# A fourth chunk with seven products in the first pairs of the late stages, and the token-side forms of these stages on GpSimd

## The chip, the core and the metric

The kernel runs on one core of a Trainium2 chip. The core has TensorE (matmuls, PE in the profile, its weight loads PEld), VectorE (DVE), ScalarE (ACT), GpSimd (POOL) and SyncE (SP), which issues most of the DMAs. The metric is the device time of one execution in microseconds; the time before is the median of three runs.

## The reference

A pre-norm encoder layer on x of 256 tokens by 2048, all in float32, batch 1, one layer:

```
h    = rms_norm(x, norm_g)
proj = h @ w_in                    # cut into q, k, v, o, za, gates, xb, zb, ga, gb
ya   = mlstm(q, k, v, gates, both directions) * head_g * sigmoid(o) * silu(za)
yb   = rglru(conv(xb), both directions) * silu(zb)
merged = sigmoid(ga) * (ya @ w_branch_a) + sigmoid(gb) * (yb @ w_branch_b)
out  = rms_norm(x + merged @ w_out, final_g)
```

w_branch_a, w_branch_b, w_out and the blocks of w_in for ga and gb are all 2048 by 2048. What is changed concerns the four products with w_branch_b, gb, ga and w_branch_a, in this order: the late stages, called WB, GB, GA and WA here.

## The kernel before

**A product in three matmuls.** Each float32 value is split into a high part (a cast to the matmul type) and a low part (the value less the high one). A product of activations a (hi) and b (lo) with weights wh and wl is three matmuls: a·wh (L174), a·wl (L176), b·wh (L177). The activations are prepared once; the weights come from memory in chunks of 128 partitions by 1024 columns (two k tiles of a block of 512 output columns) and are split on the way: a DMA into a raw buffer (L133, SyncE), a cast on ScalarE (L140), a subtraction on VectorE (L141).

**Pairs.** `pair` computes two blocks of 512 columns together, over eight chunks of k (kq 0 to 7), placed at eight places in the order of the work. Each late stage has 2048 columns, so two pairs; they are called first and second pair. A chunk is done in one of two ways:
- plain (`plain`): for each of the two blocks a load, a cast, a subtraction, and 12 matmuls (two k tiles, two halves of the tokens, three matmuls): 24 matmuls a place.
- products (`products`): the 2x2 scheme with seven products in place of eight: 7x3 = 21 matmuls. It takes two loads (L190, L191), four sums of weights on VectorE (L199, L200, L203, L204, 512 columns each, into the buffers t), casts on ScalarE of b (512 columns) and of three chunks of 1024 columns (the two sums and the second block itself, all L180), and their low parts on VectorE (L181). On the token side it needs a form.

The tuples S_… give the chunks of a stage's first and second pair that use products, and L_… the places at which these chunks are put; the other chunks fill the other places in order.

**The end of a pair.** Four of the seven products go to auxiliary banks of PSUM (aux), the rest to the banks of the pair (acc). Behind the last product place the four are folded into the outputs by a copy on ScalarE (L252) and four additions on VectorE (L253 to L256). Places up to the last product place are done for both blocks together; the places behind it are done for one block first and then for the other. At the end of each block its bank is added (L262) and the stage's epilogue runs.

**Forms.** `make_form` (L271 to L285) builds what the products need of a chunk's activations: the sum of high and low part where the full value is no longer there (L277, 512 columns, for h and ya), four sums of 128 columns (L280 to L283) in a temporary tile xp, of which there is one, then a cast on ScalarE (L284) and the low part (L285, 512 columns). All of it but the cast is on VectorE. There are seven such forms for the late stages: three of yb (b forms, from sg, while sg is at hand), one of h (the other two that GB and GA use, of chunks 4 and 0, were made for earlier stages and stay in the slots F4 and F0), three of ya. They lie in four slots of the tile PT.

**Buffers.** Weight chunks go through six raw buffers, four high and four low ones, used in turn; b goes through two, and each t through one. A load into a raw buffer waits until the subtraction that read the buffer six loads before is done.

**What sets the order.** The program is written in the order of the work, but a list scheduler orders the instructions of each engine. Loads, casts, subtractions and sums of weights stand in `urgent()` blocks, which raise their priority, earlier written ones first. Each engine then runs its instructions in that order, and waits at the first one whose operands or buffer aren't ready.

Of the kernel before, what the change touches and what calls it, by code (L numbers as in the profile page):

```python
# [10 lines left out]
F32R = mybir.dt.float32r  # L11
AF = mybir.ActivationFunctionType
ALU = mybir.AluOpType
# [6 lines left out]
NB = 512  # L20
# [3 lines left out]
EPS = 1e-6  # L24
NEG = -1e30

S_WB, S_GB, S_GA, S_WA = [((0, 2, 4), (0, 2, 4))] * 4
S_OZ = (((4, 0), (2, 4)), ((4,), (1,)), ((4, 0), (2, 5)), ((4, 0), (0, 2)))
S_V = (((4,), (4,)), ((4,), (4,)))
S_WO = (0, 1, 2, 4)  # L30
L_WB, L_GB, L_GA, L_WA = ((0, 2, 4), (0, 2, 4)), ((0, 2, 4), (0, 2, 4)), ((0, 2, 4), (0, 2, 4)), ((0, 2, 4), (1, 3, 5))
L_WO = (0, 2, 4, 6)
H_FORMS = (4, 0)
PLAN = (dict(Y=('c0', '', '', 'c1',),
# [12 lines left out]
def f(ap):  # L47
    return ap.bitcast(F32)
# [3 lines left out]
def hybrid_encoder(ctx: ExitStack, tc: tile.TileContext, x, xt, pk, bif, fg, wg, wi, wr, wa, wb, wo, out):  # L52
    nc = tc.nc
    pe, act, dve, pool, sp = nc.tensor, nc.scalar, nc.vector, nc.gpsimd, nc.sync
# [10 lines left out]
    def name(n):  # L65
        uid[0] += 1
        return f"{n}_{uid[0]}"
# [4 lines left out]
    def sl(tag, dt=F32, cols=4096):  # L72
        return slot.tile([P, cols], dt, tag=tag, name=name("s" + tag))
# [41 lines left out]
    def drain():  # L115
        while queue or any(lanes):
            tick()
        lanes.clear()
# [149 lines left out]
    def halves(t, i):  # L268
        return t[:, i * 1024:i * 1024 + NB], t[:, i * 1024 + NB:(i + 1) * 1024]

    def make_form(fm, full=None, parts=None, temp=None):  # L271
        u = xp.rearrange("p a b -> p (a b)") if temp is None else temp
        if full is None:
            full = u[:, NB:2 * NB]
            hi, lo = parts
            v = full if len(hi.shape) == 2 else full.rearrange("p (k s) -> p k s", s=S)
            dve.tensor_add(v, f(hi), f(lo))  # L277
        a11, a21, a12, a22 = [full[:, i * P:(i + 1) * P] for i in range(4)]
        s1, s2, s3, s4 = [u[:, i * P:(i + 1) * P] for i in range(4)]
        dve.tensor_add(s1, a21, a22)  # L280
        dve.tensor_sub(s2, s1, a11)
        dve.tensor_sub(s3, a11, a21)
        dve.tensor_sub(s4, a12, s2)  # L283
        act.copy(fm[0], u[:, :NB])  # L284
        dve.tensor_sub(fm[1], u[:, :NB], f(fm[0]))  # L285

    def block_first(src, xhi, xlo, pre=()):
        ps, _ = acc_pair()
# [17 lines left out]
    def half_tr(src, half, after=None, turn=False):  # L306
        ps, both = acc_pair()
        for kq in range(4):
            tick()
            hi, lo = load_chunk(src[half * 4 + kq])  # L310
            tiles = [(kq * 4 + kk, m, kk * S + m * P) for kk in range(4) for m in range(2)]
            for high in (False, True) if turn and kq % 2 else (True, False):
                for k, m, o in tiles:
                    if high:
                        pe.matmul(ps[m], hi[:, o:o + P], hl_t[:, 2 * k * S:2 * (k + 1) * S],  # L315
                                  start=(k == 0), stop=(turn and k == KT - 1), skip_group_check=True)
                    else:
                        pe.matmul(ps[m][:, :S], lo[:, o:o + P], hhi(k * S, (k + 1) * S),  # L318
                                  start=False, stop=(not turn and k == KT - 1), skip_group_check=True)
            if after:  # L320
                after(kq)
        return both.rearrange("p (m q s) -> p m q s", m=2, q=2)
# [467 lines left out]
    def h_parts(kq):  # L790
        h4 = hl_t[:, kq * 4 * S:(kq + 1) * 4 * S].rearrange("p (k q s) -> p k q s", q=2, s=S)
        return [h4[:, :, q, :] for q in range(2)]

    def forms_h(kq):
        make_form(hf[kq], parts=h_parts(kq), temp=rg["hs"][:, 3072:])
# [94 lines left out]
    yah, yal = Cols([yas["h"]], 4096), Cols([yas["l"]], 4096)  # L890
    ybh, ybl = [], []
    fslot = {}
    fm_t = []

    def form(x, kq, i, **kw):
        fslot[x, kq] = halves(fm_t[0], i)
        make_form(fslot[x, kq], **kw)

    def h_form(kq, i):
        form("h", kq, i, parts=h_parts(kq))  # L900

    def ya_form(kq, i):
        form("a", kq, i, parts=[t(kq * NB, (kq + 1) * NB) for t in (yah, yal)])

    def forms(x):
        return {kq: v for (n, kq), v in fslot.items() if n == x}
# [3 lines left out]

    k_yb, k_h, k_ya = (sorted(set(sum(v, ()))) for v in (S_WB, S_GB + S_GA, S_WA))
    k_h = [kq for kq in k_h if kq not in hf]
    early = [lambda kq=kq, i=i: h_form(kq, i) for kq, i in zip(k_h, (3, 0, 1))]
    early += [lambda kq=kq, i=i: ya_form(kq, i) for kq, i in zip(k_ya[:1], (3, 0, 1)[len(early):])]

    for j in range(4):
        for i in range(2):
            both = half_tr(wi[BLK_ZB + j], i)
            if i == 0:
                zt = hp.tile([P, 2 * NB], F32, tag="zz" if j else "vhi", name=name("zt"))  # L920
                sg = hp.tile([P, 2 * NB], F32, tag="to" if j else "vlo", name=name("sg"))
            fold(zt[:, i * NB:(i + 1) * NB], both)
        act.activation(sg, zt, AF.Silu)
        dve.tensor_mul(sg, sg, hs[:, j * 1024:(j + 1) * 1024])
        ybh.append(sl(f"C{j}", F32R, 1024))
        ybl.append(sl(f"D{j}", F32R, 1024))
        act.copy(ybh[j], sg)
        dve.tensor_sub(ybl[j], sg, f(ybh[j]))
        if j == 0:
            fm_t.append(sl("PT", F32R))  # L930
        if j == 0:
            drain()
        for kq in (2 * j, 2 * j + 1):
            if kq in k_yb:
                form("b", kq, k_yb.index(kq), full=sg[:, (kq % 2) * NB:(kq % 2 + 1) * NB])
        if j == 1:
            early[0]()
    ybh, ybl = Cols(ybh, 1024), Cols(ybl, 1024)
    nb11 = [0]

# [6 lines left out]
    sgv = [sgb[:, j * 1024:(j + 1) * 1024] for j in range(4)]  # L947
    for p in range(2):
        pair((wb[2 * p], wb[2 * p + 1]), ybh, ybl, forms("b"), S_WB[p], sgv[2 * p:2 * p + 2], b11, lambda jj: None, None, L_WB[p])
    for fn in early[1:]:  # L950
        fn()
    for p in range(2):
        gb = [sl(f"D{2 * p + i}", F32, 1024) for i in range(2)]

        def epi_gb(jj, p=p, gb=gb):
            act.activation(gb[jj], gb[jj], AF.Sigmoid)
            dve.tensor_mul(sgv[2 * p + jj], sgv[2 * p + jj], gb[jj])

        pair((wi[BLK_GB + 2 * p], wi[BLK_GB + 2 * p + 1]), hhi, hlo, forms("h"), S_GB[p], gb, b11, epi_gb, None, L_GB[p])
    ga = []  # L960
    for p in range(2):
        ga += [sl(f"C{2 * p + i}", F32, 1024) for i in range(2)]
# [2 lines left out]
            act.activation(ga[2 * p + jj], ga[2 * p + jj], AF.Sigmoid)  # L965

        pair((wi[BLK_GA + 2 * p], wi[BLK_GA + 2 * p + 1]), hhi, hlo, forms("h"), S_GA[p], ga[2 * p:], b11, epi_ga, None, L_GA[p])
    for i, kq in enumerate(k_ya[1:]):
        ya_form(kq, 1 + i)

    m_t = sl("HL", F32R, 8192)
    mh, ml = Cols([m_t[:, :4096]], 4096), Cols([m_t[:, 4096:]], 4096)
# [53 lines left out]
    for kq in S_WO:  # L1026
        make_form(mf_[kq], parts=[t(kq * NB, (kq + 1) * NB) for t in (mh, ml)])
# [15 lines left out]
    for tb, a, b, col in ((0, 0, NB, 3), (1, 0, S, 3), (1, S, NB, 4)):  # L1043
        ps = aux()[:, :b - a]
        for k in range(KT):
            hi, lo = ch[k // KC]
# [11 lines left out]
        v = y[:, tb * D + 3 * NB + a:(tb + 1) * D]  # L1058
        dve.tensor_mul(v, v, fgs[:, 3 * NB + a:])
        for i, (a, b) in enumerate(((0, S), (NB, 2 * NB), (S, NB), (2 * NB, 3 * NB), (3 * NB, D))):  # L1060
            v = y[:, tb * D + a:tb * D + b]
# [68 lines left out]
```

## Time and profile before

| | |
|---|---|
| median of 3 runs (lowest, highest) | 1013.25 us (1013.14, 1013.77) |
| span of the profiled execution | 1012.2 us |
| the median less that span | 1.05 us |
| instructions in the profile | 13718 |
| TensorE instructions (PE) | 5045 |
| DMA read from memory | 196.33 MB, 196 GB/s over the span |
| GpSimd busy | 18.6 us in 37 instructions |

The profile is of one execution. In a timeline each row has the start, the duration, the engine (SPq is the queue of DMA issues on SyncE), the line, the operation, out<-in by the program's names with shapes, and in brackets the idle time ahead of it with what ended it. Durations of back-to-back instructions overlap a little, so a pitch is read from the difference of two starts. The end of a matmul is modelled (0.39 us each); the pitch is what counts. Names of the rows: raw, whi and wlo are the buffers of weights, b is the cast and low part of the first quarter of a product chunk, t the sums of weights, acc and aux the PSUM banks, sF and sPT the slots with forms, sHL the tile of h, sD the outputs of a pair.

### The profile page before, as it was taken

How to read it: one execution, taken by the hardware profiler on the slowest of the kernel's cores; microseconds unless marked ns; L12 is line 12 of the kernel's file. 1: busy time of each engine (PE TensorE's matmuls, PEld its weight loads, DVE VectorE, ACT ScalarE, POOL GpSimd, SP SyncE). 2: the span in 40 equal slices, each digit the busy share in tenths (PEclk: the TensorE clock that was granted, in tenths of full speed). 3: DMA queues.
4: the chain of work that ended last, by engine and by line, in shares of the span. 5: the costliest groups of instructions: out<-in, count | busy, mean ns of one | idle time of the engine just before them, and what ended most of it. 6: DMA issues, size and time to landing. Idle time of an engine off the chain costs nothing.

```text
span 1012.2 us, 13718 instructions
## 1 busy us (share of the span) xinstructions
PE 1003.0 (99%) x5045; PEld 853.2 (84%) x5045; DVE 875.8 (87%) x1167; ACT 628.6 (62%) x825; POOL 18.6 (2%) x37
## 2 busy tenths in 40 slices
PE   9999999999999999999999999999999999999997
PEld 9888988888888888888888888888888888888886
DVE  6687898889769888997697888998898988999996
ACT  7546477756695786667955564655655656455562
POOL 1000000001001000000100000000000000000000
PEclk9999999999999999999999999999999999999999
DMA  9765446565555565657466466666566656568452
GB/s 349 263 208 157 160 153 198 173 213 197 167 190 167 177 197 184 210 167 227 146 199 208 155 208 188 212 212 201 187 216 200 219 177 212 184 217 336 161 200 83
DMA packets 56387, 199.32 MB, mean 197 GB/s; under 512 B 6400, under 2 KB 7424, under 8 KB 55936
## 3 DMA queue, kind: packets, MB, share of 16 engines
q1 hardware_dynamic: 55456, 197.13, 58.9%
q10 hardware_dynamic: 864, 1.32, 0.4%
q8 instruction: 39, 0.64, 0.3%
q14 instruction: 28, 0.23, 0.1%
HBM read 196.33 MB, written 2.10 MB: 196 GB/s over the span
## 4 chain that ended last, share of the span: by engine, by line
PE 97%; DVE 1%; DMA 1%; ACT 0%; issue 0%; ACTq 0%; SPq 0%; DVEq 0%
PE acc L176 17%; PE acc L177 17%; PE acc L174 17%; PE acc L315 16%; PE acc L318 8%; PE aux L176 3%; PE aux L174 3%; PE aux L177 3%; PE aux L855 1%; PE aux L721 1%; PE aux L720 1%; PE aux L719 1%; PE aux L1053 1%; PE aux L1052 1%; PE aux L1051 1%; PE acc L156 1%
## 5 line engine op out<-in xcount | busy, mean ns | idle before, releaser
L140 ACT CAST whi<-raw 128x1024 fp32r<-128x1024 f32 (+1 forms) x284 | 294.8, 1046 | 196.0 <-PE acc L177 99.7
L141 DVE TENSOR_TENSOR wlo<-raw,whi 128x1024 fp32r<-128x1024 f32 (+1 forms) x284 | 341.5, 1213 | 76.2 <-ACT whi L140 74.4
L176 PE MATMUL acc<-wlo,sHL 128*128 128x512 f32 x554 | 215.9, 390 | 0.0
L177 PE MATMUL acc<-whi,sHL 128*128 128x512 f32 x554 | 215.8, 390 | 0.0
L174 PE MATMUL acc<-whi,sHL 128*128 128x512 f32 x554 | 213.3, 390 | 0.0
L315 PE MATMUL acc<-sHL,whi 128*128 128x512 f32 x704 | 175.9, 393 | 0.0
L315 PEld LDWEIGHTS acc<-sHL,whi 128*128 128x128 f32 x704 | 127.4, 189 | 23.5
L174 PEld LDWEIGHTS acc<-whi,sHL 128*128 128x128 f32 x554 | 104.0, 188 | 21.2
L176 PEld LDWEIGHTS acc<-wlo,sHL 128*128 128x128 f32 x554 | 104.1, 188 | 21.0
L177 PEld LDWEIGHTS acc<-whi,sHL 128*128 128x128 f32 x554 | 104.0, 188 | 20.9
L318 PEld LDWEIGHTS acc<-sHL,wlo 128*128 128x128 f32 x704 | 95.3, 190 | 6.0
L180 ACT CAST whi<-t 128x1024 fp32r<-128x1024 f32 x70 | 73.5, 1051 | 42.9 <-PE acc L177 13.9
L318 PE MATMUL acc<-sHL,wlo 128*128 128x256 f32 x704 | 99.0, 283 | 0.0
L181 DVE TENSOR_TENSOR wlo<-t,whi 128x1024 fp32r<-128x1024 f32 x70 | 85.5, 1222 | 9.0 <-ACT whi L180 8.5
L180 ACT CAST whi<-raw 128x1024 fp32r<-128x1024 f32 x37 | 39.0, 1053 | 27.6 <-PE acc L177 16.9
L181 DVE TENSOR_TENSOR wlo<-raw,whi 128x1024 fp32r<-128x1024 f32 x37 | 45.2, 1222 | 8.7 <-ACT whi L180 8.7
L180 ACT CAST b<-raw 128x512 fp32r<-128x512 f32 x28 | 17.4, 621 | 39.2 <-DMA raw<-wi 16.5
L176 PE MATMUL acc<-wlo,sC 128*128 128x512 f32 x92 | 35.9, 390 | 0.4 <-DVE wlo L141 0.4
L176 PE MATMUL acc<-wlo,sA 128*128 128x512 f32 x92 | 36.0, 392 | 0.0
L177 PE MATMUL acc<-whi,sD 128*128 128x512 f32 x92 | 35.8, 389 | 0.0
L177 PE MATMUL acc<-whi,sB 128*128 128x512 f32 x92 | 35.8, 389 | 0.0
L174 PE MATMUL acc<-whi,sC 128*128 128x512 f32 x92 | 35.3, 389 | 0.0
(361 smaller groups left out, 1589.1 us busy)
## 6 DMA issues: line engine op xcount, KB each, us to landing
raw<-wi SPq DMA_DIRECT2D x254, 512.0 KB, 4.2
raw<-wb SPq DMA_DIRECT2D x32, 512.0 KB, 4.1
raw<-wa SPq DMA_DIRECT2D x32, 512.0 KB, 4.0
raw<-wo SPq DMA_DIRECT2D x32, 512.0 KB, 4.8
raw<-wr SPq DMA_DIRECT2D x8, 512.0 KB, 4.0
sB<-x SPq DMA_DIRECT2D x4, 512.0 KB, 7.7
sA<-x SPq DMA_DIRECT2D x1, 2048.0 KB, 7.9
sA<-xt SPq DMA_DIRECT2D x7, 256.0 KB, 6.7
```

The source lines that it names most:

```text
L140: last_copy[0] = act.copy(hi[:, r], raw[:, r]).ins
L141: last_sub[0] = dve.tensor_sub(lo[:, r], raw[:, r], f(hi[:, r])).ins
L156: pe.matmul(ps[tb], a, wl, start=False, stop=False)
L174: pe.matmul(ps, a, wh, start=id(ps) not in began, stop=False)
L176: pe.matmul(ps, a, wl, start=False, stop=False)
L177: pe.matmul(ps, b, wh, start=False, stop=stop)
L180: act.copy(hi, v)
L181: dve.tensor_sub(lo, v, f(hi))
L315: pe.matmul(ps[m], hi[:, o:o + P], hl_t[:, 2 * k * S:2 * (k + 1) * S], start=(k == 0), stop=(turn and k == KT - 1), skip_group_check=True)
L318: pe.matmul(ps[m][:, :S], lo[:, o:o + P], hhi(k * S, (k + 1) * S), start=False, stop=(not turn and k == KT - 1), skip_group_check=True)
L719: pe.matmul(dst, whi[:, o:o + P], xh[:, r], start=True, stop=False)
L720: pe.matmul(dst, whi[:, o:o + P], xl[:, r], start=False, stop=False)
```

## The change

First pairs of the four late stages use products in four chunks (0, 2, 4, 6) in place of three, at places 0, 2, 4 and 6. Second pairs keep three, at places 1, 3 and 5 in place of 0, 2 and 4 (WA's second pair stood there already). make_form gets an argument that says which engine runs its additions and subtractions; for the forms of the late stages it is GpSimd, for the others, and for those of the last stage, still VectorE. There are now ten late forms. The cast in a form stays on ScalarE. The forms of h (chunks 2 and 6) are made behind WB's pairs as before behind slot 0 and 1 of PT, those of ya for chunks 0 and 2 behind each of GB's pairs, and those of ya for chunks 4 and 6 behind GA's pairs, in the slots F0 and F4, whose forms of h are done with by then.

```
-S_WB, S_GB, S_GA, S_WA = [((0, 2, 4), (0, 2, 4))] * 4
+S_WB, S_GB, S_GA, S_WA = [((0, 2, 4, 6), (0, 2, 4))] * 4
-L_WB, L_GB, L_GA, L_WA = ((0, 2, 4), (0, 2, 4)), ((0, 2, 4), (0, 2, 4)), ((0, 2, 4), (0, 2, 4)), ((0, 2, 4), (1, 3, 5))
+L_WB, L_GB, L_GA, L_WA = [((0, 2, 4, 6), (1, 3, 5))] * 4
...
-    def make_form(fm, full=None, parts=None, temp=None):
+    def make_form(fm, full=None, parts=None, temp=None, by=None):
+        by = by or dve
...
-            dve.tensor_add(v, f(hi), f(lo))
+            by.tensor_tensor(v, f(hi), f(lo), op=ALU.add)
...
-        dve.tensor_add(s1, a21, a22)
-        dve.tensor_sub(s2, s1, a11)
-        dve.tensor_sub(s3, a11, a21)
-        dve.tensor_sub(s4, a12, s2)
+        by.tensor_tensor(s1, a21, a22, op=ALU.add)
+        by.tensor_tensor(s2, s1, a11, op=ALU.subtract)
+        by.tensor_tensor(s3, a11, a21, op=ALU.subtract)
+        by.tensor_tensor(s4, a12, s2, op=ALU.subtract)
         act.copy(fm[0], u[:, :NB])
-        dve.tensor_sub(fm[1], u[:, :NB], f(fm[0]))
+        by.tensor_tensor(fm[1], u[:, :NB], f(fm[0]), op=ALU.subtract)
...
-        make_form(fslot[x, kq], **kw)
+        make_form(fslot[x, kq], by=pool, **kw)
...
-    early = [lambda kq=kq, i=i: h_form(kq, i) for kq, i in zip(k_h, (3, 0, 1))]
-    early += [lambda kq=kq, i=i: ya_form(kq, i) for kq, i in zip(k_ya[:1], (3, 0, 1)[len(early):])]
...
-        if j == 1:
-            early[0]()
...
-    for fn in early[1:]:
-        fn()
+    for i, kq in enumerate(k_h):
+        h_form(kq, i)
...
         pair((wi[BLK_GB + 2 * p], wi[BLK_GB + 2 * p + 1]), hhi, hlo, forms("h"), S_GB[p], gb, b11, epi_gb, None, L_GB[p])
+        ya_form(k_ya[p], 2 + p)
...
-    for i, kq in enumerate(k_ya[1:]):
-        ya_form(kq, 1 + i)
+    for kq, slot_ in zip(k_ya[2:], H_FORMS[::-1]):
+        fslot["a", kq] = halves(sl(f"F{slot_}", F32R, 1024), 0)
+        make_form(fslot["a", kq], by=pool, parts=[t(kq * NB, (kq + 1) * NB) for t in (yah, yal)])
```

The scheduler makes its order anew, so more moves than these lines. TensorE at the hand-over from GB's first pair to its second, before: acc_1343 is the bank of the first pair's second block, the aux banks and acc_1429 belong to the second pair, whi_1437 and whi_1439 are the two sums of product place 0, and b11_1458 is the b of product place 2. Numbers count the tiles in the order in which the program asks for them.

```order
L174 MATMUL acc_1343_6230<-whi_1424_6544,sHL_5_90 128x512
L176 MATMUL acc_1343_6230<-wlo_1425_6545,sHL_5_90 128x512
L177 MATMUL acc_1343_6230<-whi_1424_6544,sHL_5_90 128x512
L174 MATMUL aux_1444_6594<-whi_1437_6579,sF0_295_1520 128x512
L176 MATMUL aux_1444_6594<-wlo_1438_6580,sF0_295_1520 128x512
L177 MATMUL aux_1444_6594<-whi_1437_6579,sF0_295_1520 128x512
L174 MATMUL aux_1445_6595<-whi_1437_6579,sF0_295_1520 128x512
L176 MATMUL aux_1445_6595<-wlo_1438_6580,sF0_295_1520 128x512
L177 MATMUL aux_1445_6595<-whi_1437_6579,sF0_295_1520 128x512
L174 MATMUL aux_1446_6596<-whi_1439_6585,sF0_295_1520 128x512
L174 MATMUL acc_1429_6566<-whi_1439_6585,sHL_5_90 128x512
L174 MATMUL aux_1443_6593<-b11_1458_6658,sHL_5_90 128x512
```

The same place after: acc_1347 is the bank of the first pair's second block at place 7, acc_1437 that of the second pair; whi_1441 is the plain chunk at place 0, whi_1453 and whi_1455 the sums of the product chunk at place 1, and b11_1474 the b of the product chunk at place 3.

```order
L174 MATMUL acc_1347_6246<-whi_1432_6570,sHL_5_90 128x512
L176 MATMUL acc_1347_6246<-wlo_1433_6571,sHL_5_90 128x512
L177 MATMUL acc_1347_6246<-whi_1432_6570,sHL_5_90 128x512
L174 MATMUL aux_1461_6664<-whi_1453_6648,sF0_295_1520 128x512
L174 MATMUL aux_1460_6663<-whi_1453_6648,sF0_295_1520 128x512
L174 MATMUL aux_1459_6662<-b11_1474_6727,sHL_5_90 128x512
L174 MATMUL aux_1462_6665<-whi_1455_6654,sF0_295_1520 128x512
L176 MATMUL aux_1460_6663<-wlo_1454_6649,sF0_295_1520 128x512
L177 MATMUL aux_1460_6663<-whi_1453_6648,sF0_295_1520 128x512
L176 MATMUL aux_1461_6664<-wlo_1454_6649,sF0_295_1520 128x512
L177 MATMUL aux_1461_6664<-whi_1453_6648,sF0_295_1520 128x512
L174 MATMUL acc_1437_6599<-whi_1441_6602,sHL_5_90 128x512
```

Matmuls of the product chunk at place 1, and the first one on the b of place 3, now stand ahead of the plain chunk at place 0.

ScalarE after, at the same place: casts of the last two chunks of the first pair (whi_1427, whi_1432), of the two blocks at place 0 (whi_1441, whi_1445), then of the product chunks.

```order
L140 CAST whi_1427_6549<-raw_1426_6548 128x1024
L140 CAST whi_1432_6570<-raw_1431_6569 128x1024
L140 CAST whi_1441_6602<-raw_1440_6601 128x1024
L140 CAST whi_1445_6620<-raw_1444_6619 128x1024
L180 CAST whi_1453_6648<-t_1451_6644 128x1024
L180 CAST b11_1474_6727<-raw_1472_6723 128x512
L180 CAST whi_1455_6654<-t_1452_6645 128x1024
```

The cast of b11_1474 stands between those of the two sums of place 1, and its buffer raw_1472 is the one six loads behind raw_1440 (the loads between are 1444, the two of place 1, and the two of place 2).

VectorE after, there, from the last chunk of the first pair (wlo_1433) on:

```order
L141 TENSOR_TENSOR wlo_1433_6571<-raw_1431_6569,whi_1432_6570 128x1024
L200 TENSOR_TENSOR t_1451_6644<-raw_1449_6638,raw_1448_6637 128x512
L254 TENSOR_TENSOR sD0_1344_6243<-aux_1362_6274,sD1_1345_6244 128x512
L141 TENSOR_TENSOR wlo_1442_6603<-raw_1440_6601,whi_1441_6602 128x1024
L203 TENSOR_TENSOR t_1452_6645<-t_1451_6644,raw_1448_6637 128x512
L141 TENSOR_TENSOR wlo_1446_6621<-raw_1444_6619,whi_1445_6620 128x1024
L255 TENSOR_TENSOR sD1_1345_6244<-aux_1361_6273,sD1_1345_6244 128x512
L256 TENSOR_TENSOR sD1_1345_6244<-aux_1361_6273,sD0_1344_6243 128x512
L204 TENSOR_TENSOR t_1452_6645<-raw_1449_6638,t_1452_6645 128x512
L181 TENSOR_TENSOR wlo_1454_6649<-t_1451_6644,whi_1453_6648 128x1024
L262 TENSOR_TENSOR sD0_1344_6243<-sD0_1344_6243,acc_1346_6245 128x1024
```

Between the last low half of the first pair and the low half that frees raw_1440 (wlo_1442) stand now two additions of 512 columns, and the additions of the fold are spread over the hand-over. In the order before, the fold's last addition (L256) stood five rows ahead of the last low half of the first pair (wlo_1425), and the sums for product place 0 of the second pair were begun between them.

On SyncE one row moves past others: the load of the final norm's gains (fg) into PT, which waits for the last reader of PT's forms, stood behind all loads of wa and three of wo, and stands now ahead of the last two of wa.

## The prediction

> **What bounds the kernel now.** The page comes first: which engine is full, and which one the chain that ended last runs through.
>
> ```profile
> PE 1003.0 (99%) x5045; PEld 853.2 (84%) x5045; DVE 875.8 (87%) x1167; ACT 628.6 (62%) x825; POOL 18.6 (2%) x37
> PE 97%; DVE 1%; DMA 1%; ACT 0%; issue 0%; ACTq 0%; SPq 0%; DVEq 0%
> ```
>
> TensorE is full and carries 97% of the chain, so a matmul less is time less as long as nothing else makes TensorE wait. The change reaches from about 520 us (GpSimd's first forms) to about 920 us, so the second view is the table of windows for that stretch; its columns are length, then busy time and instructions of PE, PEld, DVE, ACT and POOL. The third is the list of waits of TensorE there.
>
> ```profile
> 600.00:920.00 320.00, 319.63 (x1417) 264.25 (x1416) 288.99 (x331) 179.12 (x190) 0.00 (x0) 1.00 0.62 206
> sum 400.00, PE 399.63 PEld 333.84 DVE 357.01 ACT 224.76 POOL 0.00; mean PE 199.81 PEld 166.92 DVE 178.51 ACT 112.38 POOL 0.00
> PE acc L176 <- DVE wlo L141: 0.4, 1, 0.4
> ```
>
> TensorE idles 0.4 us of 400, at the granted clock 1.00. VectorE is next with 357 of 400, 43 us of slack in all. A mean of 43 says nothing of one hand-over between pairs, so those are followed one by one below.
>
> **Matmuls.** A plain chunk place is 2x12 matmuls, a product place 7x3. Four pairs get a fourth product place: 4x(24-21) = 12 matmuls fewer. The timeline of TensorE gives the pitch; between these two rows lie 23 steps:
>
> ```profile
> 745.79 0.39 PE L176 MATMUL acc<-wlo,sHL 128*128 128x512 f32 x1
> ...
> 751.01 0.39 PE L174 MATMUL aux<-whi,sF 128*128 128x512 f32 x1
> ```
>
> (751.01-745.79)/23 = 0.227 us, so 12 matmuls are **-2.7 us**, 0.27% of the kernel. That is all the change can gain, and little above the 0.2% that a measurement of this kernel can tell from no change.
>
> **VectorE.** Pitches, from starts in its timeline:
>
> ```profile
> 740.46 2.36 DVE L141 TENSOR_TENSOR wlo<-raw,whi 128x1024 fp32r<-128x1024 f32 x2
> 742.73 0.69 DVE L203 TENSOR_TENSOR t<-t,raw 128x512 f32<-128x512 f32 x1
> 743.33 1.22 DVE L262 TENSOR_TENSOR sD<-sD,acc 128x1024 f32<-128x1024 f32 x1
> ...
> 549.60 0.29 DVE L280 TENSOR_TENSOR xp<-xp 128x128 f32<-128x128 f32 x1
> 549.81 0.28 DVE L282 TENSOR_TENSOR xp<-xp 128x128 f32<-128x128 f32 x1
> ```
>
> 1024 columns take (742.73-740.46)/2 = 1.135 us, 512 take 0.60, 128 take 0.21. A product place costs 5x0.60+3x1.135 = 6.4, a plain one 2x1.135 = 2.3: four exchanges add 4x4.1 = 16.5. Seven forms leave VectorE: four steps and the low half, 4x0.21+0.60 = 1.44, and four of them 0.60 more for L277: 3x1.44+4x2.04 = 12.5. Net +4.0 in a stretch that loses 2.7 us and has 43 idle. Summed, VectorE fits, and ScalarE (225 of 400 busy) does as well. By sums alone the whole 2.7 us would arrive.
>
> **The hand-over from a first pair to its second.** Here I find the cost. Before, three plain places (5, 6, 7) follow a first pair's last product place, done for one column block and then the other; VectorE and ScalarE work ahead in them. After, only place 7 follows product place 6, the next pair has one plain place (0), and then products at place 1. How far ahead is VectorE two chunks behind a last product place? Before shows just that behind product place 4 of the GB stage's second pair, with the fold's additions in between as they will be at place 7. Starts of VectorE, and of TensorE's first use of the two low halves:
>
> ```profile
> 731.71 1.23 DVE L141 TENSOR_TENSOR wlo<-raw,whi 128x1024 fp32r<-128x1024 f32 x1 [1.72 <-ACT whi L140]
> ...
> 733.46 1.22 DVE L141 TENSOR_TENSOR wlo<-raw,whi 128x1024 fp32r<-128x1024 f32 x1
> 734.59 0.69 DVE L254 TENSOR_TENSOR sD<-aux,sD 128x512 f32<-128x512 f32 x1
> ```
> ```profile
> 734.24 0.39 PE L176 MATMUL acc<-wlo,sHL 128*128 128x512 f32 x1
> ...
> 736.96 0.39 PE L176 MATMUL acc<-wlo,sHL 128*128 128x512 f32 x1
> ```
>
> The second low half ends at 733.46+1.22 = 734.68 and is used at 736.96: 2.3 us ahead (up to 2.9 if VectorE lags less). Let T be the time at which TensorE has finished the first pair of the GB stage after the change. The last chunk's low half is first used 11 matmuls = 2.5 us before T, so it is ready at about T-4.8 to T-5.4. By the order of VectorE there follow L200 (0.60), L254 (0.60) and the low half of the next pair's place 0 (1.135): done at T-2.4 to T-3.0, say T-2.75. That subtraction frees the raw buffer into which block 0 of the product chunk at place 3 is loaded (six buffers in turn). In TensorE's order the first matmul on that chunk's b (b11_1474) has come forward to the third place behind T, and in ScalarE's order the cast of b stands ahead of that of whi_1455, which TensorE wants as its fourth matmul, at T+0.68. From issue of such a load to the cast of b, and the casts behind it, before shows (SyncE, then ScalarE):
>
> ```profile
> 700.18 0.33 SPq L190 DMA_DIRECT2D raw<-wi  x1
> ...
> 712.43 0.33 SPq L190 DMA_DIRECT2D raw<-wi  x1
> ...
> 741.71 0.33 SPq L190 DMA_DIRECT2D raw<-wi  x1
> ```
> ```profile
> 703.96 0.62 ACT L180 CAST b<-raw 128x512 fp32r<-128x512 f32 x1 [1.52 <-DMA raw<-wi]
> ...
> 706.86 1.03 ACT L180 CAST whi<-t 128x1024 fp32r<-128x1024 f32 x1
> ...
> 716.54 0.62 ACT L180 CAST b<-raw 128x512 fp32r<-128x512 f32 x1 [2.31 <-DMA raw<-wi]
> 717.07 1.05 ACT L180 CAST whi<-t 128x1024 fp32r<-128x1024 f32 x1
> ...
> 745.16 0.62 ACT L180 CAST b<-raw 128x512 fp32r<-128x512 f32 x1 [1.25 <-DMA raw<-wi]
> ```
>
> 3.45, 3.78 and 4.11 us, each time with ScalarE idle for the transfer. So b's cast starts at T-2.75+3.78 = T+1.03, whi_1455 follows 0.53 later and takes 1.05: T+2.6. TensorE waits 2.6-0.68 = **1.9 us** (1.35 with the early ends, 2.6 with the late ones). The low half wlo_1454, also wanted there, comes at T+1.9 by VectorE's order (4.67 of pitches behind T-2.75) and hides in that wait, and so does L262. Before has cover at this spot: there T is 709.53, the cast for the second sum of place 0 ends at 706.86+1.03 = 707.89, and TensorE takes it up at
>
> ```profile
> 709.53 0.39 PE L174 MATMUL aux<-whi,sF 128*128 128x512 f32 x1
> ...
> 710.89 0.39 PE L174 MATMUL aux<-whi,sF 128*128 128x512 f32 x1
> ```
>
> 3.0 us later. The order stands alike at the WB and GA hand-overs: 1.9 each. At WA only b itself (b11_1835, third matmul, T+0.45) has moved forward: T+1.03+0.62-0.45 = 1.2 (0.6 to 1.9). Four hand-overs: 3x1.9+1.2 = **+6.9** (4.65 to 9.7; zero if VectorE reaches place 7 some 2 us earlier than at place 5 before). Second pair to the next stage's first: here two places (6, 7), done block by block, follow the last product place instead of three; the lead shrinks and no order row puts a load in the way: 0, at most 1 for the three of them.
>
> **GpSimd's forms.** Ten forms are 40 operations of 128 and 16 of 512 columns. No two-input operation of such a size by GpSimd stands in the trace; the nearest are a one-input cast, and small operations that wait for VectorE:
>
> ```profile
> L443 POOL CAST st__166<-ident 128x512 fp32r<-128x512 f32 x2 | 1.2, 614 | 0.0
> ```
> ```profile
> 237.25 2.86 POOL L860 TENSOR_SCALAR sq<-sq 128x1 f32<-128x1 f32 x1 [200.26 <-ACT to L859]
> ...
> 240.83 0.19 POOL L860 TENSOR_SCALAR sq<-sq 128x1 f32<-128x1 f32 x1
> ```
> ```profile
> 237.10 2.36 DVE L141 TENSOR_TENSOR wlo<-raw,whi 128x1024 fp32r<-128x1024 f32 x2
> 239.37 0.69 DVE L199 TENSOR_TENSOR t<-raw 128x512 f32<-128x512 f32 x1
> 240.78 0.75 DVE L862 SCALAR_TENSOR_TENSOR to<-aux,sq,zz 128x512 f32<-128x512 f32 x1 [0.72 <-POOL sq L861]
> ```
>
> The same 128x1 operation took 0.19 us beside a VectorE operation with PSUM among its inputs, and 2.86 through three back-to-back operations on SBUF. So GpSimd's forms will stretch; a form takes from 4x0.19+0.61 (free) to 5x2.86 = 14 us. Most are wanted tens of us later; ScalarE's cast of a form, in its queue, is what can hold up the weight casts behind it. That decides for the last b form (place 6 of WB), whose end falls into VectorE's run without a gap,
>
> ```profile
> 587.49 1.22 DVE L924 TENSOR_TENSOR sg<-sg,sE 128x1024 f32<-128x1024 f32 x1
> ...
> 600.20 0.69 DVE L204 TENSOR_TENSOR t<-raw,t 128x512 f32<-128x512 f32 x1
> ```
>
> and perhaps for a ya form. I take +0.8 (0 to 5), near the lower end because GpSimd got through within three VectorE operations in the row above. [...]
>
> **Others at nothing.** The fg load into PT now stands on SyncE ahead of two wa loads, and waits for PT's last reader, product place 3 of WA's second pair; the first of these loads is used 69 matmuls (15.7 us) later against about 6 us of load, cast and subtraction. Without that cover it would cost those 6. ScalarE's extra casts are hidden by its idle 44%.
>
> **Sum and rivals.** -2.7+6.9+0.8 = +5.0. The profiled execution has 1012.2 us of span and 1.05 around it to the median of 1013.25, so the sum is put on the median: **1018.2 us**. Own range: -2.7+4.65+0 = 1015.2 to -2.7+9.7+1.0 = 1021.3. Chance 0.52.
>
> Second case, faster: VectorE keeps its lead through product place 6 (it has lost the forms, 12.5 us) and the loads land in 3.45, so that all four waits come to under 0.7 us together. It decides at 2 us of lead per hand-over: low half of place 0 ready at T-4.7 instead of T-2.75. For it: 43 us of idle VectorE, 3.0 us of cover before. Against: VectorE at place 5 had only 1.3 and 2.3 us of lead, with slack elsewhere. Time 1013.25-2.7 = 1010.5; chance 0.17.
>
> Third case: part of this, waits of 0.7 to 4.7 us together, eats the gain: 1011.2 to 1015.2, 1013.2 in the middle; chance 0.23.
>
> Fourth, GpSimd blocks VectorE. From the last b form on, 13 operations of 512 and 28 of 128 run, at 0.61 and 0.19 to 0.61 each 13 to 25 us, on a VectorE with 320-289 = 31 us idle less three to four exchanges' 12 to 16, plus about 8 for the forms gone there: some 24. It decides when they fall into stretches without gaps; at 7 us over, 1025. No VectorE operation in the trace is lengthened. Chance 0.08.
>
> The range takes in the first three and leaves out the fourth: 1010.4 to 1021.5. Faster by over 0.2% (2.0 us): the second case and a sliver of the third, 0.18. Within: 0.22. Slower: 0.60.
>
> **What would show it.** Right: 12 matmuls fewer, and four new waits of TensorE on whi or b (ScalarE behind a DMA) of 1 to 3 us, one in each late stage, with a cast of b that waits for its load just ahead. The one of the GB stage falls near 710 us. Wrong: no waits there and 2.7 us gained (second case); waits on low halves from VectorE all over the stretch, with gaps ended by GpSimd or longer operations (fourth); waits behind the cast of a form at about 600 us above 1 us (my GpSimd term).

## The result and the profile after

The changed kernel takes 1039.56 us (median of four, 1037.94 to 1040.38) against 1013.19 for the kernel before in the same runs: a ratio of 1.0253, with a 95% interval of 1.0238 to 1.0267. It is slower, as forecast, but by 26.4 us where 5.0 were forecast, and outside the range. Executions at a granted clock of about 0.65 (1434 to 1436 us) are left out of every time and ratio here and below. The profiled execution has a span of 1036.2 us, 24.0 more than before. The engine line of the page:

```profile
PE 1012.3 (98%) x5033; PEld 853.1 (82%) x5033; DVE 900.1 (87%) x1152; ACT 634.7 (61%) x836; POOL 86.9 (8%) x93
```

The 12 matmuls are gone (5045 to 5033). VectorE has 15 instructions fewer and is busy 24.3 us longer, where the forecast had +4.0. The waits of TensorE between 500 and 960 us (engine, tile and line, whom it waited for, us in all, times, longest); before had 0.4 us there:

```profile
PE aux L174 <- ACT b L180: 8.0, 4, 2.4
PE acc L176 <- DVE wlo L181: 1.8, 3, 0.9
PE aux L174 <- ACT whi L180: 1.5, 4, 0.4
PE aux L176 <- DVE wlo L181: 1.5, 1, 1.5
PE aux L174 <- DVE sE L256: 1.3, 1, 1.3
PE acc L176 <- DVE wlo L141: 0.8, 2, 0.5
PE aux L174 <- DVE sD L256: 0.5, 1, 0.5
PE acc L174 <- DVE sC L262: 0.2, 1, 0.2
```

The first row is the forecast wait: one at each of four hand-overs, on the b of place 3. With the others it makes 15.6 us. The hand-over of GB, with TensorE, then ScalarE, then SyncE's queue, shows the wait in the form that was worked out:

```profile
724.55 0.50 PE L174 MATMUL aux<-b,sHL 128*128 128x512 f32 x1 [2.25 <-ACT b L180]
725.49 0.50 PE L174 MATMUL aux<-whi,sF 128*128 128x512 f32 x1 [0.45 <-ACT whi L180]
```
```profile
723.88 0.62 ACT L180 CAST b<-raw 128x512 fp32r<-128x512 f32 x1 [3.39 <-DMA raw<-wi]
724.40 1.04 ACT L180 CAST whi<-t 128x1024 fp32r<-128x1024 f32 x1
```
```profile
718.55 0.33 SPq L190 DMA_DIRECT2D raw<-wi  x1
719.15 0.33 SPq L191 DMA_DIRECT2D raw<-wi  x1
```

ScalarE has idled 3.39 us for the load, and TensorE waits for its cast. But from issue to cast the load takes 723.88-718.55 = 5.3 us, not 3.8. At WB and WA, where the waits were longest, it is the same, but not at GA (WB, GA, WA in this order):

```profile
625.19 0.33 SPq L190 DMA_DIRECT2D raw<-wb  x1
...
805.32 0.33 SPq L190 DMA_DIRECT2D raw<-wi  x1
...
892.40 0.33 SPq L190 DMA_DIRECT2D raw<-wa  x1
```
```profile
630.37 0.62 ACT L180 CAST b<-raw 128x512 fp32r<-128x512 f32 x1 [5.10 <-DMA raw<-wb]
...
809.13 0.62 ACT L180 CAST b<-raw 128x512 fp32r<-128x512 f32 x1 [2.32 <-DMA raw<-wi]
...
897.53 0.62 ACT L180 CAST b<-raw 128x512 fp32r<-128x512 f32 x1 [4.30 <-DMA raw<-wa]
```

5.2, 3.8 and 5.1 us. Two things came on top. The first is TensorE's clock. The table of windows (after the engines' busy times come the granted clock, the DMA share and GB/s) for stretches behind or around three waits:

```profile
631.60:635.20 3.60, 3.21 (x8) 2.53 (x9) 3.44 (x5) 1.01 (x2) 0.00 (x0) 0.53 0.04 15
683.00:686.20 3.20, 3.20 (x9) 2.24 (x8) 3.20 (x4) 0.00 (x0) 0.00 (x0) 0.50 0.70 197
722.00:726.00 4.00, 1.31 (x5) 0.65 (x4) 4.00 (x6) 2.11 (x3) 0.00 (x0) 1.00 0.71 264
```

Behind WB's hand-over and at 683 us the granted clock is about a half for some 3.2 us, behind GB's it is not. The matmuls at WA, which had the same:

```profile
898.80 0.63 PE L176 MATMUL aux<-wlo,sPT 128*128 128x512 f32 x1
899.22 0.63 PE L177 MATMUL aux<-whi,sPT 128*128 128x512 f32 x1
```

They start 0.427 us apart instead of 0.227; with about eight such in each of the three places it is 3x8x0.2 = 4.8 us. In each of the three the slow stretch lasts about 3.2 us. The waits ahead differ: 2.25 us at GB, with none just ahead of it, was followed by the full clock (1.00); 2.38 us with 1.30 just ahead at WB, 2.35 with 0.55 just ahead at WA, and 1.50 and 0.91 ahead of 683 us were followed by about half of it. The length of one wait doesn't decide it: in the run with the forms on VectorE (below), single waits of 2.24 and 2.48 us were followed by the full clock, and three in a row of 0.17, 1.09 and 0.44 us, at GA, by 3.1 us at a granted clock of 0.50. What does decide it is open.

The second is GpSimd beside VectorE, from 644 us on, where 24 operations of five forms run one after the other:

```profile
649.94 2.15 POOL L278 TENSOR_TENSOR xp<-sA,sB 128x512 f32<-128x512 f32 x1
654.09 1.45 POOL L286 TENSOR_TENSOR sPT<-xp,sPT 128x512 fp32r<-128x512 f32 x1 [2.00 <-ACT sPT L285]
```
```profile
650.87 1.77 DVE L203 TENSOR_TENSOR t<-t,raw 128x512 f32<-128x512 f32 x1
652.57 1.21 DVE L141 TENSOR_TENSOR wlo<-raw,whi 128x1024 fp32r<-128x1024 f32 x1
653.70 0.68 DVE L204 TENSOR_TENSOR t<-raw,t 128x512 f32<-128x512 f32 x1
654.30 2.32 DVE L141 TENSOR_TENSOR wlo<-raw,whi 128x1024 fp32r<-128x1024 f32 x1
```

L203 takes 1.77 us beside GpSimd's L278 where L204, begun while GpSimd is idle, takes 0.68; L141 takes 2.32 instead of 1.21. This was my fourth case. A wait of TensorE on a low half, with VectorE's row first:

```profile
678.00 2.31 DVE L181 TENSOR_TENSOR wlo<-t,whi 128x1024 fp32r<-128x1024 f32 x1
680.36 0.50 PE L176 MATMUL aux<-wlo,sF 128*128 128x512 f32 x1 [1.50 <-DVE wlo L181]
```

Together: -2.7 of matmuls, 15.2 of new waits and 4.8 of slow matmuls give 17.3 of the 24.0 us. The starts of TensorE's matmuls place nearly all of it, since they also hold the waits too short to be listed and, at each listed wait, the 0.16 to 0.27 us by which the step across it is longer than pitch and wait together. Where a step from one start to the next is longer than 0.26 us, what it has over the pitch of 0.227 comes to 27.2 us between 520 and 965 us, against 1.2 before; less the 2.7 that is 23.3 of the 24.0. Of the 27.2, 16.8 lie at the four hand-overs from a first pair to its second and 7.1 at the three from a second pair to the next stage's first (5.1 of them from WB to GB, at the end of GpSimd's row of forms, the slow stretch at 683 us included); the rest is spread out.

### The profile page after: what moved, and what is told of

Read it like the earlier page. It is cut to its first block, busy times and chain, and to the rows that moved or that the text cites. A ratio compares the mean times of both kernels' runs of the same rounds, so it can differ in the third digit from the quotient of the medians.

```text
span 1036.2 us, 13780 instructions
## 1 busy us (share of the span) xinstructions
PE 1012.3 (98%) x5033; PEld 853.1 (82%) x5033; DVE 900.1 (87%) x1152; ACT 634.7 (61%) x836; POOL 86.9 (8%) x93
## 5 line engine op out<-in xcount | busy, mean ns | idle before, releaser
L141 DVE TENSOR_TENSOR wlo<-raw,whi 128x1024 fp32r<-128x1024 f32 (+1 forms) x276 | 338.7, 1235 | 74.6 <-ACT whi L140 72.9
L140 ACT CAST whi<-raw 128x1024 fp32r<-128x1024 f32 (+1 forms) x276 | 285.2, 1045 | 158.9 <-PE acc L177 77.7
L176 PE MATMUL acc<-wlo,sHL 128*128 128x512 f32 x542 | 211.9, 391 | 1.0 <-DVE wlo L181 0.9
L177 PE MATMUL acc<-whi,sHL 128*128 128x512 f32 x542 | 211.4, 390 | 0.0
L174 PE MATMUL acc<-whi,sHL 128*128 128x512 f32 x542 | 208.3, 391 | 0.0
L176 PEld LDWEIGHTS acc<-wlo,sHL 128*128 128x128 f32 x542 | 101.9, 188 | 23.3 <-DVE wlo L141 1.4
L174 PEld LDWEIGHTS acc<-whi,sHL 128*128 128x128 f32 x542 | 102.1, 188 | 20.9
L177 PEld LDWEIGHTS acc<-whi,sHL 128*128 128x128 f32 x542 | 101.8, 188 | 20.4
L180 ACT CAST whi<-t 128x1024 fp32r<-128x1024 f32 x78 | 82.0, 1052 | 57.8 <-PE acc L177 26.2
L181 DVE TENSOR_TENSOR wlo<-t,whi 128x1024 fp32r<-128x1024 f32 x78 | 97.8, 1260 | 5.3 <-ACT whi L180 5.0
L180 ACT CAST whi<-raw 128x1024 fp32r<-128x1024 f32 x41 | 43.1, 1050 | 25.9 <-PE acc L177 13.2
L181 DVE TENSOR_TENSOR wlo<-raw,whi 128x1024 fp32r<-128x1024 f32 x41 | 52.7, 1285 | 2.7 <-ACT whi L180 2.7
L861 POOL TENSOR_SCALAR sq<-sq 128x1 f32<-128x1 f32 x8 | 7.4, 923 | 427.4 <-ACT to L860 427.0
L199 DVE TENSOR_TENSOR t<-raw 128x512 f32<-128x512 f32 x37 | 26.8, 723 | 12.8 <-DMA raw<-wi 5.5
```

The lines of the kernel that those rows point to most:

```text
L140: last_copy[0] = act.copy(hi[:, r], raw[:, r]).ins
L141: last_sub[0] = dve.tensor_sub(lo[:, r], raw[:, r], f(hi[:, r])).ins
L174: pe.matmul(ps, a, wh, start=id(ps) not in began, stop=False)
L176: pe.matmul(ps, a, wl, start=False, stop=False)
L177: pe.matmul(ps, b, wh, start=False, stop=stop)
L180: act.copy(hi, v)
```

## The experiments

Theory H is the prediction's (a late load at the hand-over from a first pair to a second), theory G is that GpSimd's forms block VectorE, and theory L that the new arrangement simply gives VectorE and ScalarE too much to do. Differences are to the kernel before on the same chip. Waits are TensorE's between 520 and 960 us in the profiled execution; "on b" are those of L174 on ScalarE's b.

| kernel | us | ratio to before (95%) | more, us | waits | of it on b |
|---|---|---|---|---|---|
| as changed | 1039.56 | 1.0253 (1.0238 to 1.0267) | 26.4 | 15.6 | 8.0 |
| forms on VectorE | 1028.44 | 1.0132 (1.0113 to 1.0152) | 14.6 | 9.3 | 6.6 |
| before, forms on GpSimd | 1014.81 | 1.0014 (1.0004 to 1.0024) | 1.0 | 0.5 | 0 |
| places 0, 1, 3, 5 | 1030.33 | 1.0164 (1.0148 to 1.0179) | 16.5 | 10.0 | 0.4 |
| seven raw buffers | 1027.99 | 1.0139 (1.0124 to 1.0154) | 14.1 | 7.9 | 1.3 |
| seven buffers, forms on VectorE | 1025.82 | 1.0125 (1.0108 to 1.0142) | 12.1 | | |
| the same again | 1023.39 | 1.0096 (1.0077 to 1.0115) | 9.8 | 6.6 | 1.0 |
| before, seven buffers | 1015.97 | 1.0022 (1.0013 to 1.0031) | 2.3 | 0.5 | 0 |
| seven buffers, b forms on GpSimd | 1022.67 | 1.0089 (1.0076 to 1.0103) | 9.0 | 3.5 | 1.1 |
| places 0, 1, 3, 5, forms on VectorE | 1025.77 | 1.0115 (1.0100 to 1.0130) | 12.1 | 8.1 | 0 |
| seven buffers, h forms on VectorE | 1023.93 | 1.0102 (1.0088 to 1.0116) | 10.3 | 5.5 | 0 |
| before, second pairs shifted | 1018.65 | 1.0052 (1.0037 to 1.0066) | 5.1 | 0.4 | 0 |
| b of place 1 used again | 1032.17 | 1.0185 (1.0168 to 1.0202) | 18.7 | 9.9 | 0 |
| the same, forms on VectorE | 1024.89 | 1.0110 (1.0095 to 1.0125) | 11.4 | 7.4 | 0 |

**The late forms back on VectorE.** In the changed kernel:

```
-        make_form(fslot[x, kq], by=pool, **kw)
+        make_form(fslot[x, kq], **kw)
...
-        make_form(fslot["a", kq], by=pool, parts=...)
+        make_form(fslot["a", kq], parts=...)
```

> The changed kernel with its ten late forms back on VectorE; chunks and places stay as changed. Theory H (the hand-over from a first pair to its second waits for the b of place 3, whose load starts late): the waits of TensorE on b stay, each about 1 us shorter, since by VectorE's order the low half that frees the buffer comes about 1.2 us earlier; 1022 to 1028 us, with four waits on b or whi behind a load. Theory G (GpSimd's forms block VectorE and delay everything): the lengthened VectorE operations go and with them the waits; 1010 to 1016 us.

14.6 us over before: 11.8 of the 26.4 hang on the engine of the forms, the other 14.6 don't. The waits on b stay, four of them and hardly shorter:

```profile
PE aux L174 <- ACT b L180: 6.6, 4, 2.5
PE aux L174 <- ACT whi L180: 1.1, 2, 0.7
PE acc L174 <- DVE sD L262: 1.0, 1, 1.0
```

Neither theory alone has it all; the time is just above H's range, and G is worth much more than the 0.8 us that I gave it. VectorE is busy 896.2 us here and 900.1 with the forms on GpSimd: taking ten forms away from it made it busier. But not all of the 11.8 us arises while GpSimd runs. Compared matmul by matmul (the first of one with the first of the other, and so on; both have 5033), the changed kernel falls behind this run by 4.1 us between 600 and 653 us and by 4.0 between 653 and 705, wins back 3.4 between 753 and 847, and loses 4.9 between 847 and 943; GpSimd runs nothing of its forms from 602.4 to 643.9 us, nor after 843.5.

**Only the forms on GpSimd.** The kernel before with `by=pool` for its late forms, nothing else.

> The kernel before, with nothing but its seven late forms moved to GpSimd; chunks and places as before. Theory H: the places have not moved, so no new waits at the hand-overs; 1012.5 to 1015 us. Theory G: seven of ten forms run on GpSimd, so about seven tenths of the 26 us; 1025 us or more, with waits on VectorE's low halves and sums.

Same to 0.14%, though GpSimd is as slow here (from 560 us on L286 takes 1.29 to 2.38 us, in the changed kernel 1.29 to 2.29); VectorE is busy 873.7 us against 875.8 before, so of the 12.5 us that the prediction puts at its forms, all but 2.1 came back as longer operations. The windows around the forms, before's arrangement with GpSimd first, the changed kernel second:

```profile
565.00:643.90 78.90, 78.90 (x375) 66.11 (x374) 74.07 (x76) 45.72 (x51) 20.52 (x17) 1.00 0.57 188
643.90:682.00 38.10, 38.10 (x170) 31.56 (x169) 35.35 (x40) 20.73 (x23) 8.10 (x6) 1.00 0.61 199
```
```profile
565.00:643.90 78.90, 74.37 (x342) 60.64 (x341) 70.30 (x73) 41.26 (x48) 18.56 (x15) 0.98 0.54 177
643.90:682.00 38.10, 35.59 (x152) 27.64 (x150) 37.26 (x33) 20.46 (x24) 29.47 (x24) 1.00 0.48 153
```

GpSimd runs as long in the first stretch of both kernels (20.5 and 18.6 us); in the second it runs 8.1 us against 29.5, and VectorE is then busy 37.3 of 38.1. G by each form is out. Whether GpSimd costs more in the changed kernel because more of its operations stand together there or because VectorE has less lead, these two runs don't separate.

**Other places.** `L_... = [((0, 1, 3, 5), (1, 3, 5))] * 4` in the changed kernel: two plain places behind the last product place.

> The changed kernel with the four product chunks of a first pair at places 0, 1, 3 and 5 in place of 0, 2, 4 and 6, so that two plain places stand behind the last one; forms stay on GpSimd. TensorE's order has no matmul on the b of place 3 at the hand-over any more. Theory H: the waits on b at the four hand-overs (17 us with what follows them) go, the rest stays; 1020 to 1026 us. Theory G: nothing but order moves, 1035 us or more.

The waits on b fall from 8.0 to 0.4 us and the time by 9.9, from 26.4 to 16.5 over before. That the waits go is as H has it, but the time stays 4 us above its range. Others came instead, inside the pairs, where two product places stand together and at 644 to 690 us:

```profile
PE aux L176 <- DVE wlo L181: 3.9, 5, 1.0
PE aux L174 <- ACT whi L180: 3.3, 4, 1.6
```

**Seven raw buffers.** In the changed kernel:

```
-            raw = wp.tile([P, KC * NB], F32, tag="raw", name=name("raw"), bufs=6)
+            raw = wp.tile([P, KC * NB], F32, tag="raw", name=name("raw"), bufs=7)
...
-                r1, r2 = [wp.tile(..., bufs=6) for _ in range(2)]
+                r1, r2 = [wp.tile(..., bufs=7) for _ in range(2)]
```

To make room, the tile ng of an earlier stage takes the memory of another, ab; that is part of this edit in all runs with seven buffers.

> The changed kernel with seven raw buffers in place of six (a small tile of the gates' preparation shares its memory with another to make room). The load of the b of place 3 then waits for the low half before the one that it waits for now, which is about 2.3 us earlier. Theory H: each wait on b shrinks by about 2.3 us, at GB and GA to nothing; 1024 to 1030 us. Theory G: no difference, 1036 us or more.

12 us less, within H's range, and the waits on b fall to 1.3 us, though the edit has a price of its own (below). What is left is on VectorE, by the timeline most of it between 644 and 690 us, beside GpSimd:

```profile
PE acc L176 <- DVE wlo L141: 2.1, 3, 1.0
PE aux L176 <- DVE wlo L181: 1.7, 1, 1.7
PE aux L174 <- ACT b L180: 1.3, 1, 1.3
```

**Seven buffers and all forms on VectorE**, run twice.

> The changed kernel with seven raw buffers and its ten late forms on VectorE. Both causes are taken out together. If the late load of b and GpSimd's blocking are the two causes (H and G together): the 2.7 us of matmuls arrive, less some 1 to 3 us of small waits that are left at the hand-overs; 1011 to 1015 us. If the fourth product place costs by VectorE's and ScalarE's mere load (theory L): most of the 14.6 us that the changed places cost with the forms on VectorE stays, 1022 us or more.

> The run with seven raw buffers and all late forms on VectorE once more, for the profile that it lacks. Its time of 1027 us stood against H and G together. If H holds with another order at fault, the waits lie at single hand-overs (GB above all, where TensorE's order takes b and the second sum of later chunks early); if theory L holds, they are spread over the pairs, on VectorE's low halves.

Neither time comes near 1011 to 1015: the expectation of H and G together fell, and both lie in L's range. In the second run's profile the longest waits lie at the hand-overs of WB and GB and are on L262:

```profile
PE acc L174 <- DVE sE L262: 1.7, 1, 1.7
PE acc L174 <- DVE sD L262: 1.7, 1, 1.7
PE aux L174 <- ACT whi L180: 1.2, 3, 0.5
PE aux L174 <- ACT b L180: 1.0, 1, 1.0
```

TensorE waits for the second pair's bank, which VectorE frees late. So with the load out of the way at most hand-overs, VectorE's own lag there comes last: not L as I put it (the waits are not spread over the pairs), but not the load alone either.

**Seven buffers in the kernel before.**

> The kernel before with seven raw buffers and nothing else. It waits 0.5 us in all in its late stages, so there is nothing to win there: within 0.2% of before, 1011.5 to 1014.5 us, by every theory. It says whether the seventh buffer alone is worth anything.

2.3 us slower, against every theory's expectation. So the runs with seven buffers carry about 2 us of another origin. Compared matmul by matmul, TensorE is already 1.8 of the 2.0 us of span behind at 527 us, ahead of the late stages; whether the seventh buffer or the shared tile does it was not tried.

**Only the b forms on GpSimd**, with seven buffers.

> The changed kernel with seven raw buffers, its four b forms on GpSimd, and the six forms of h and ya on VectorE. Theory G says that GpSimd costs where it runs without pause beside a VectorE that has no slack, which was at 644 to 680 us by the h and ya forms; the b forms ran before it. So near the run with all forms on VectorE: 1011 to 1017 us. If GpSimd costs by each form, four tenths of the 11 us that ten forms cost: 4 us above that run.

The lowest time with four product chunks in this series, a little under the runs with all forms on VectorE (9.0 against 9.8 and 12.1 us over before), and 5 us under all forms on GpSimd. The b forms cost nothing that shows; the time itself missed its range, as that of the run with all forms on VectorE had. With seven buffers all ten forms on GpSimd cost 2.0 to 4.3 us more than on VectorE (14.1 against 12.1 and 9.8), not 11.8.

**Places 0, 1, 3, 5 with forms on VectorE.**

> The changed kernel with first pairs' product places at 0, 1, 3 and 5 and all late forms on VectorE, six raw buffers. No b is wanted early at the hand-over from a first to a second pair, so without GpSimd only the waits inside the pairs that two neighbouring product places bring are left (3 to 6 us in the run with GpSimd): 1013 to 1019 us by H and G together. By theory L 1024 us or more.

12.1 us over before without a wait on b. The expectation of H and G fell here too, and the time is in L's range: neighbouring product places come with more waits than I allowed, on ScalarE's and VectorE's parts of the products.

**The forms of h on VectorE, the others on GpSimd**, seven buffers.

> The changed kernel with seven raw buffers, the two forms of h on VectorE and the eight of yb and ya on GpSimd. By TensorE's order the GB hand-over is the one of the run with seven buffers and all forms on GpSimd, which had no wait there, and two of the five forms that GpSimd ran without pause at 644 to 680 us are gone. Theory G with H: about half of the 8.5 us of waits of that stretch go, and nothing comes back at the hand-overs; 1019 to 1025 us, 3 to 8 us under that run. Theory L (VectorE's load decides): VectorE gets 4 us more to do in the stretch where it has no slack; 1028 us or more.

3.8 us under all forms on GpSimd (10.3 against 14.1 over before), as G with H had it, and 4 us more of work for VectorE made nothing worse.

**Only the shift of the second pairs.** In the kernel before, `L_... = [((0, 2, 4), (1, 3, 5))] * 4`.

> The kernel before with the second pairs' products at places 1, 3 and 5 in all late stages, three chunks with products in every pair, all forms on VectorE. Here a first pair keeps three plain places behind its last product place. Theory H as I put it (the hand-over costs because only one plain place is left): no waits on b, 1012.5 to 1015 us. If it is the shift of the second pairs that costs (two plain places left at their end, one plain place ahead of the first product): up to half of the 14.6 us, 1017 to 1021 us.

5.1 us: the shift has a price without the fourth chunk. The time lies in the range of the second expectation, that the shift of the second pairs costs, and outside that of H as I had put it. The profiled execution (span 1015.7, 3.5 over before) lists only 0.4 us of waits; the starts of TensorE's matmuls place 2.5 us in longer steps, 1.5 of it from 669 to 685 us, where GB's first pair follows WB's second. Where the other 1.0 us goes is open.

**The b of place 1 used again at place 3**, in late second pairs, with the forms on GpSimd and on VectorE:

```
-                bh, bl = b11()
-                split(bh, bl, r1[:, lf])
+                if places == (1, 3, 5) and len(bb) == 1:
+                    bb.append(bb[0])
+                else:
+                    bb.append(b11())
+                    split(*bb[-1], r1[:, lf])
+                bh, bl = bb[-1]
```

> The changed kernel without one thing: in the late second pairs the product chunk at place 3 takes the b of place 1 again, so its own b is neither cast nor split nor waited for (its load is still made, for the sums). The output of these stages is not the reference's; only the time counts. TensorE's order at the GB hand-over is the changed one, word for word, less the matmul on that b. Theory H: the four waits on b and the slow matmuls behind two of them go, about 10 to 14 us: 1026 to 1030 us. Theory G or L: the four casts and subtractions less are worth under 3 us; 1036 us or more.

> The same omission (place 3 of the late second pairs takes the b of place 1 again) in the run with all late forms on VectorE and six raw buffers, which took 1028.4 us and waited 8 us on b. Theory H: 1017 to 1022 us. Theory L (the load of VectorE and ScalarE): 1026 us or more.

7.7 and 3.2 us less (18.7 against 26.4 over before, 11.4 against 14.6): between the two theories. (The waits on b that the second expectation puts at 8 us were 6.6.) All waits on ScalarE's b are gone, but other waits took part of their place; with the forms on GpSimd:

```profile
PE aux L177 <- DVE wlo L182: 3.0, 3, 1.5
PE aux L175 <- ACT whi L181: 2.4, 3, 0.9
PE acc L177 <- DVE wlo L141: 1.3, 3, 0.5
PE acc L175 <- DVE sD L267: 1.3, 1, 1.3
```

(The lines stand one to five further down here: L182 is the low half of a product chunk, L267 the addition of the bank.) So the load of b is the last of several late things, and VectorE's low half and the second sum's cast stand close behind it, with waits of up to 1.5 and 0.9 us. The engine of the forms is worth 7.3 us here (18.7 against 11.4), 11.8 as changed, 4.4 at places 0, 1, 3 and 5, and 1.0 in the kernel before.

## Why the prediction was right and wrong

**Matmuls.** -2.7 us: right, 12 fewer.

**The hand-over.** The mechanism was right: four waits on b, behind a load that starts when the low half of place 0 has freed its buffer, and they go when the load can start earlier or isn't needed. Its size was wrong. The step that failed is "T-2.75+3.78", T being the end of the first pair:

| | forecast | WB | GB | GA | WA |
|---|---|---|---|---|---|
| load issued, us ahead of T | 2.75 | 1.27 | 3.13 | 2.68 | 2.03 |
| from issue to b's cast | 3.78 | 5.18 | 5.33 | 3.81 | 5.13 |
| lost by TensorE, by the starts | 1.9 (WA 1.2) | 6.5 | 3.2 | 2.2 | 4.9 |
| of it matmuls at half clock | 0 | 1.6 | 0 | 0 | 1.6 |

At GA both terms came out as forecast, and so, within 0.3 us, did what TensorE lost. At three hand-overs the load took 1.4 to 1.6 us longer, and at WB and WA VectorE freed the buffer later too. Together with the slow matmuls these make nearly all of the 16.8 us that stand in place of 6.9. The three rows behind the 3.78 were all of one stage; before already held a longer one, and behind loads issued alike (the next two 0.6 and 1.7 us later, as at all four hand-overs) it held a short one as well, each with the cast that waited for it:

```profile
616.75 0.33 SPq L190 DMA_DIRECT2D raw<-wb  x1
...
825.19 0.33 SPq L190 DMA_DIRECT2D raw<-wa  x1
```
```profile
622.91 0.62 ACT L180 CAST b<-raw 128x512 fp32r<-128x512 f32 x1 [4.13 <-DMA raw<-wb]
...
828.61 0.63 ACT L180 CAST b<-raw 128x512 fp32r<-128x512 f32 x1 [1.73 <-DMA raw<-wa]
```

6.2 and 3.4 us. So the spacing of the loads doesn't tell how long one takes; why they differ is open. The step also took the load as the only thing late: at GB "wlo_1454 ... hides in that wait" holds, but other operands are close behind, which is why taking b away gave 3 to 8 us and not all.

**Second pair to the next first pair.** "0, at most 1" failed: by the starts it is 7.1 us at the three of them. The two waits on low halves at 680 and 683 us are at the first, beside GpSimd. With the forms on VectorE 1.6 us are left there and 1.6 from GB to GA. The shift of the second pairs alone costs 5.1 us, for which the sum had no term.

**GpSimd's forms.** +0.8, with 0 to 5 as bounds: wrong; it is 11.8 us in the changed arrangement. Two steps failed. "Most are wanted tens of us later" looked at when forms are needed and not at when GpSimd does them: from 644 us on, operations of five forms stand together, behind one that had waited 41.57 us for ScalarE's cast into its slot. And I counted GpSimd's waiting and ScalarE's casts, not VectorE's waiting; the row that I took as evidence (2.86 us) shows GpSimd's side alone. That VectorE is lengthened in turn, which the fourth case supposed, no row in the prediction shows; the changed kernel does: between 520 and 960 us VectorE's operations of 512 columns without a PSUM bank take 1.02 us on average where GpSimd runs beside them for over 0.3 of their time, and 0.68 where it is idle. The fourth case, 1025 us at a chance of 0.08, came on top of the first, and I had treated the two as alternatives. They do more than add: with the forms on VectorE taking b away gives 3.2 us, with b away moving the forms gives 7.3, and both together 15.0 (26.4 against 11.4). That each takes from the same lead is how I read it; no run shows it by itself.

**The clock.** No term at all. The trace of before has one wait of 0.4 us in this stretch and couldn't show matmuls that start 0.427 us apart instead of 0.227, as they did behind the waits at WB, at WA and ahead of 683 us. Of the 4.8 us, 3.2 are in the table above.

**What stays open**: why the loads at WB, GB and WA took longer than at GA, what sets off the half clock, and how the forms on GpSimd cost time at hand-overs where GpSimd is idle. Of the 14.6 us without GpSimd and the 2.7 that did not show as a gain, 3.2 go with b and 5.1 are what the shift costs by itself; if these simply add, some 9 us belong to VectorE's and ScalarE's other late operands, which no run took out one by one. No version with a fourth product chunk beat the kernel before; the best stood 9.0 us over it.

## What to carry to other kernels

Where one engine is full, a step that shortens its work by 0.3% pays only if each hand-over keeps its lead; work out for the tightest hand-over, row by row, when the last operand comes, and then ask what stands 1 or 2 us behind it. Moving work to GpSimd may not unload VectorE: here VectorE's operations beside it grew by about as much as was taken away (by all but 2.1 of 12.5 us in the kernel before, and by 3.9 more than that in the changed one), which cost 1 us in the kernel before and 2 to 12 in the changed ones. A load's time is better taken from the whole spread of a trace than from the three rows nearest by. When two rivals draw on the same slack, forecast them together and not as alternatives.

## What the hardware showed that I had not expected

An addition or subtraction of 512 columns by VectorE took up to 1.78 us beside GpSimd (L203 at 601.12 us) instead of 0.68, and one of 1024 columns up to 2.32 (L141 at 654.30) instead of 1.22; GpSimd's own ones, by two of the groups of the changed kernel (count, then busy us and mean ns),

```profile
L281 POOL TENSOR_TENSOR xp<-xp 128x128 f32<-128x128 f32 x6 | 7.0, 1165 | 0.5
L278 POOL TENSOR_TENSOR xp<-sA,sB 128x512 f32<-128x512 f32 x4 | 7.0, 1751 | 0.3
```

took 1.17 us on average for 128 columns and 1.75 for 512. The shortest of 128 columns took 0.45 us (L282 at 676.53 us, while VectorE ran L262, which has a PSUM bank among its inputs); beside L203 and L141, which have none, L284 at 668.94 us took 1.33. VectorE's additions with a PSUM bank among their inputs took no longer beside GpSimd: 0.68 us for each of four of 512 columns (L253 to L256, 664.73 to 674.25 us) and 1.21 for one of 1024 (L262 at 676.17). Of TensorE's waits, 1.30 and 2.38 us at WB, 0.55 and 2.35 at WA, and 1.50 and 0.91 ahead of 683 us were followed by about 3.2 us at half clock (0.50 to 0.53 granted), and 2.25 us at GB was followed by the full clock.
